# An encoder layer on one core: a bias table moved to the right end of memory, projection weights loaded in pairs, gate stores on another queue, keys loaded by units, and two banks for attention results

## The chip, the cores and the metric

The kernel runs on one core of a Trainium2 chip. A core has a matrix engine (PE, which loads weights, shown as PEld, and streams matmuls), three elementwise engines (DVE, ACT and POOL), and SP, which here only issues transfers (DMAs). Each engine works through its own list of instructions in order and waits on semaphores for the others. Work memory has 128 partitions; results of matmuls go to eight banks of 128 x 512 floats. The metric is the device time of one launch in microseconds (us); a launch is also profiled once, and the profile is what the times of single instructions come from.

## The reference, cut to what matters

One layer over 2048 tokens of width 1024, all in float32:

```python
h = rms_norm(x, norm_mix)
z = h @ w_in            # q_A k_A v_A | q_B k_B v_B | gate_A gate_B
y_a = windowed_gqa(q_a, k_a, v_a, sink)      # |t - s| <= 128, ALiBi, 8 heads in 2 key groups
y_b = neighborhood_attn(q_b, k_b, v_b, rpb)  # 8 x 16 window on a 32 x 64 grid, 8 heads, bias table
gates = sigmoid(concat(g_a, g_b) + b_gate)
merged = gates[:, :1024] * (y_a @ w_proj_a) + gates[:, 1024:] * (y_b @ w_proj_b)
x = x + merged @ w_out
x = x + square(relu(rms_norm(x, norm_mlp) @ w_up)) @ w_down
return rms_norm(x, norm_final)
```

## The kernel before, in words

Matmuls keep float32 accuracy with two halves: an operand is split into a rounded part and the rest, and a product is three matmuls (`mm3`, lines 202 to 204). The split is a CAST on ACT and a subtraction on DVE or POOL.

The kernel has five stages. The first (to about 540 us) multiplies by `w_in` and stores queries, keys, values and half of the gates to DRAM. The second, A, is the windowed attention: 32 units `attn_a(g, i)`, one for a key group g and a block i of 128 queries. The third, B, is the neighbourhood attention: 32 units `attn_b`, four for each of eight heads. The fourth multiplies by `w_proj_b`, merges and multiplies by `w_out`. The fifth is the feed-forward part. The change touches the second and the third, and the order of instructions is the same ahead of them and from the fourth stage's second part on.

A unit of A loads its queries (`qa`), makes scores in a bank `s` (L844, L845), adds the group's table of distances `biasa0` or `biasa1` on DVE (L846), takes exponentials on ACT, divides on POOL (L857), transposes on PE (L863, bank `pt`), splits the result into `ph` and `pl` (L867, L868) and multiplies by the values into a bank `av` (L869, L870), which ACT and DVE empty into `ya` (L872, L873). Group 1 gives the first five units, then all of group 0 runs, then the other eleven of group 1. A unit of B goes the same way with `qb`, keys `kb0` or `kb1` (by the head's parity, 2 MB in three DMAs, L1027 to L1029), values `vb0` to `vb2` (L1040), a bias made by POOL from a loaded piece `braw` (L1012, L1018), and `phb`, `plb`, `av`, `yb`.

Beside the attention PE gets filler work, in steps: `gate_tiles(f)` (128 columns of the gates for two blocks of 512 tokens, 24 matmuls a tile) and `proj_tile(f)` (128 columns of y_a @ w_proj_a for all four blocks, 12 matmuls a tile). The tiles go to a bank `mm`; a gate tile is emptied by a tanh on ACT (L470), and its store to DRAM (`zg`) is issued by ACT; a projection tile is emptied by DVE (L962), multiplied by its gate that was loaded again. The first projections need y_a as four split pages (`y_page`, one for each block of 512 tokens; L939 loads, L282 and L283 split). `paced` ties step n of the filler to a place among the units' transposes: 84 steps in A, 108 in B, of which the last 10 come behind the attention. `put` keeps a store until `flush` issues it on a queue.

The bank tags take 2 (`mm`) + 3 (`s`) + 2 (`pt`) + 1 (`av`) of the eight banks. Pools of work memory are laid from the left end and from the right end, in the order of their lists (L804, L805 for A; L993, L994 for B). B's pools reuse A's places, so a tile of B can be loaded when the last reader of what lay there is done. Before the change kb0 lies over the three `pl` tiles, free space and the end of `ka0`; `kb1` over `sa` and `ya`; `vb0` over the end of `ka1`. With the change kb0 lies over free space, `biasa1` and the end of `ka0`; `kb1` over `sa`, `ya` and `ph`; `vb0` over the end of `ka1` and the first part of `va1`.

Order is set by a scheduler of the language: it takes the program order, the waits that `issue_after` adds and its own idea of durations, and writes one list for each engine.

Of the kernel before, what the change touches and what calls it, by code (L numbers as in the profile page):

```python
# [8 lines left out]
F32 = mybir.dt.float32  # L9
F32R = mybir.dt.float32r  # L10
# [82 lines left out]
def encoder_layer(ctx, tc, x, norm_mix, w_in, b_gate, sink, rpb, w_pa, w_pb, w_out,  # L93
# [374 lines left out]
    def half_tanh(out, z, f):  # L468

        A.activation(out, z, AF.Tanh, scale=0.5, bias=bg[:, f : f + 1])  # L470
# [330 lines left out]
    s_w = ExitStack()  # L801
    wp = pools(s_w, "right", ("raw", "whl", "z"), "w")
    s_a = ExitStack()
    ap_ = pools(s_a, "left", ("dist", "sta", "qa", "biasa1", "ka1", "va1", "sa", "ya", "ph", "pl"), "a")  # L804
    ap_.update(pools(s_a, "right", ("biasa0", "va0", "ka0"), "a"))  # L805

    dist = T(ap_, [P, 384], F32, "dist", 1)
    SY.dma_start(dist, dist_a)
# [20 lines left out]
    def attn_a(g, i):  # L829
        c0, c1 = (1 if i == 0 else 0), (2 if i == 15 else 3)  # L830
        lo, hi = c0 * P, c1 * P
        n = hi - lo
        if bias_a[g] is None:
            make_bias_a(g)
        base = (i - 1) * P
        q = T(ap_, [P, 4, P], F32R, "qa", 3)
        began.append(SY.dma_start(q.bitcast(F32), qs_a[g][i // 8][:, :, i % 8]).ins)
        ka, v = kas[g], vas[g]
        s = T(ap_, [P, 4, 384], F32, "sa", 4)
        st = T(ap_, [P, 8, 4], F32, "sta", 8)  # L840
        mx, nm, sm, es, ri = (st[:, k, :] for k in range(5))
        for h in range(4):
            ps = psum("s", 3)
            PE.matmul(ps[:, :n], q[:, h, :], ka[:, 0, base + lo : base + hi], start=True, stop=False)  # L844
            PE.matmul(ps[:, :n], q[:, h, :], ka[:, 1, base + lo : base + hi], start=False, stop=True)  # L845
            V.tensor_tensor_reduce(out=s[:, h, lo:hi], in0=ps[:, :n], in1=bias_a[g][:, h, lo:hi], scale=1.0,  # L846
                                   scalar=sink_t[:, 4 * g + h : 4 * g + h + 1], op0=ALU.add, op1=ALU.max,
                                   accum_out=mx[:, h : h + 1])
        A.activation(nm, mx, AF.Copy, scale=-1.0)
        V.tensor_tensor(out=es, in0=sink_t[:, 4 * g : 4 * g + 4], in1=mx, op=ALU.subtract)  # L850
        A.activation(es, es, AF.Exp)
        for h in range(4):
            A.activation(s[:, h, lo:hi], s[:, h, lo:hi], AF.Exp, bias=nm[:, h : h + 1], accum_out=sm[:, h : h + 1])
        V.tensor_tensor(out=sm, in0=sm, in1=es, op=ALU.add)
        V.reciprocal(ri, sm)
        for h in range(4):
            G.tensor_scalar(s[:, h, lo:hi], s[:, h, lo:hi], ri[:, h : h + 1], 0.5, ALU.mult, ALU.mult)  # L857
        yield
        po = psum("av", 1)
        for c in range(c0, c1):  # L860
            pt = psum("pt", 2)
            for h in range(4):
                last = PE.transpose(pt[:, h * P : (h + 1) * P], s[:, h, c * P : (c + 1) * P], ident).ins  # L863
# [5 lines left out]
            PE.matmul(po, v[:, i - 1 + c, :], ph, start=c == c0, stop=False)  # L869
            PE.matmul(po, v[:, i - 1 + c, :], pl, start=False, stop=c == c1 - 1)  # L870
        t = T(ap_, [64, 512], F32, "ya", 2)
        A.copy(t, po[64:128, :])  # L872
        V.tensor_tensor(out=t, in0=po[0:64, :], in1=t, op=ALU.add)  # L873
# [44 lines left out]
    def gate_tiles(*fs):  # L918
        raws = [load_slice([(cols(w_in[0], O_GA + f * P), KC)]) for f in fs]
        yield  # L920
        hls = [split_slice(raw) for raw in raws]
        yield
        for b in (3, 2) if len(fs) > 1 else (2, 3):
            for f, hl in zip(fs, hls):
                ps = psum("mm", 2)
                yield from in_chunks(ps, hl, hp[b])
                z = T(wp, [P, 2, BT], F32, "z", 3)[:, 0]
                half_tanh(z, ps, f)
                A.dma_start(zg[b][f // 8][(f % 8) * P : (f % 8 + 1) * P, :], z)
                yield  # L930

    ypages = [None] * NB
# [7 lines left out]
            split(raw, halves(hi)[g], halves(lo)[g], V)  # L940
        ypages[b] = hi, lo

    def proj_tile(f):
        raw = load_slice([(cols(w_pa[0], f * P), 4)])
        yield
        hl = T(wp, [P, 2, KC, P], F32R, "whl", 2)
        split(raw[:, 0:4], hl[:, 0, 0:4], hl[:, 1, 0:4], V)
        yield
        for b in (0, 2):
            z = T(wp, [P, 2, BT], F32, "z", 3)  # L950
            for j in range(2):
                SY.dma_start(z[:, j], zg[b + j][0][f * P : (f + 1) * P, :])
            for j in range(2):
                if ypages[b + j] is None:
                    y_page(b + j)
                hi, lo = ypages[b + j]
                ps = psum("mm", 2)
                for c in range(4):
                    mm3(ps, hl[:, 0, c, :], hl[:, 1, c, :], hi[:, c], lo[:, c], c == 0, c == 3)
                    if c == 1:  # L960
                        yield
                V.scalar_tensor_tensor(out=z[:, j], in0=z[:, j], scalar=1.0, in1=ps, op0=ALU.add, op1=ALU.mult)  # L962
                put(zp[b + j][f], z[:, j])
                yield


    fill = [gate_tiles(f) for f in range(14)] + [gate_tiles(14, 15)] + [proj_tile(f) for f in range(8)]
    for n in (0, 0, 1):
        next(fill[n])
    next(fill[1])  # L970
# [15 lines left out]
    paced(fill, given, 84, 92, 12, last=True)  # L986
# [45 lines left out]
    def attn_b(n_u, h, j, k, bias):  # L1032
# [36 lines left out]
        po = psum("av", 1)  # L1069
        first = True  # L1070
        for pair in range(4):
            pt = psum("pt", 2)
# [78 lines left out]
    first_y = load_y(0)  # L1151
    for _ in range(2):
        next_y = next(first_y)
    paced(fill, given, 108, 128, 4, 10, True)
    flush(queue=SY)
    s_h.close()
    s_pp.close()
# [639 lines left out]
```

## Time and profile before

| | us |
|---|---|
| median of 3 runs | 2664.44 |
| lowest and highest | 2658.15, 2670.09 |
| the profiled execution | 2657.3 |
| its span, first to last instruction | 2655.5 |
| PE busy | 2561.9 |
| DVE busy | 1703.8 |
| ACT busy | 1308.3 |
| mean granted clock of PE | 0.988 |

The span is 1.8 us shorter than the time of the execution that it belongs to. Rows of a timeline read: start, duration, engine, line, operation, written tile <- read tiles, shape, count, and in brackets the idle time of the engine before it with what ended it. A q behind an engine's name means its sequencer, which issues DMAs or waits. The granted clock is the share of the full PE clock; at 0.5 matmuls take twice as long.

### The profile page before, as it was taken

To read this page: it belongs to the slowest core of one execution; us is meant where nothing else is said; L and a number is where in the kernel's file an instruction comes from. 1 tells how busy PE (TensorE), PEld (TensorE's weight loads), DVE (VectorE), ACT (ScalarE), POOL (GpSimd) and SP (SyncE) were. 2 spreads that over 40 slices of the span, in tenths; PEclk is the share of its full clock that TensorE was granted. 3 is DMA by queue.
4 is the path that set the end of the run, shared out by engine and by line. 5 is a ranking of instruction groups with operands and counts; after the bars stand their busy time and mean duration, and the time that the engine had idled before them with its cause. 6 is when DMAs were issued, how large, how long until landed. Compare 5 with 4: busy or idle time off the path is not lost. (4 is left out here: it accounts for less than half of the span.)

```text
span 2655.5 us, 34541 instructions
## 1 busy us (share of the span) xinstructions
PE 2561.9 (96%) x11936; PEld 2124.7 (80%) x11936; DVE 1703.8 (64%) x2700; ACT 1308.3 (49%) x2349; POOL 336.8 (13%) x460
## 2 busy tenths in 40 slices
PE   8999999989996989999999999999999999999998
PEld 6887888878875877878877888888887888888887
DVE  7857477646763556657697776776566634555766
ACT  7365465557763655622336555554444333322444
POOL 1001001043443645300000000000000000000011
PEclk9999999999998999999999999999999999999999
DMA  5768478783347888888888655854436935445555
GB/s 183 224 189 299 144 271 279 243 242 88 102 119 164 221 228 249 231 271 297 284 316 279 225 204 201 286 198 155 147 116 258 326 113 178 143 147 172 185 189 169
DMA packets 348159, 553.21 MB, mean 208 GB/s; under 512 B 30904, under 2 KB 152888, under 8 KB 345808
## 3 DMA queue, kind: packets, MB, share of 16 engines
q1 hardware_dynamic: 328912, 506.96, 59.7%
q10 hardware_dynamic: 15552, 32.51, 3.3%
q0 software_dynamic: 3520, 11.54, 1.2%
q8 instruction: 94, 1.54, 0.2%
q14 instruction: 81, 0.66, 0.1%
HBM read 364.19 MB, written 186.71 MB: 207 GB/s over the span
## 5 line engine op out<-in xcount | busy, mean ns | idle before, releaser
L287 PE MATMUL b<-dwh,dah 128*128 128x512 f32 x896 | 348.7, 389 | 0.4 <-DVE dwh L283 0.4
L288 PE MATMUL b<-dwh,dah 128*128 128x512 f32 x896 | 347.8, 389 | 0.0
L286 PE MATMUL b<-dwh,dah 128*128 128x512 f32 x896 | 338.3, 389 | 1.6 <-ACT dwh L282 1.6
L282 ACT CAST dah<-da 128x1024 fp32r<-128x1024 f32 (+1 forms) x128 | 120.9, 945 | 367.7 <-PE b L288 245.4
L286 PE MATMUL zb<-zh,zwhl 128*128 128x512 f32 x728 | 285.6, 392 | 6.2 <-ACT zb L532 2.4
L287 PE MATMUL zb<-zh,zwhl 128*128 128x512 f32 x728 | 285.2, 392 | 0.0
L288 PE MATMUL zb<-zh,zwhl 128*128 128x512 f32 x728 | 283.8, 391 | 0.9 <-DVE zwhl L283 0.8
L283 DVE TENSOR_TENSOR dah<-da,dah 128x1024 fp32r<-128x1024 f32 (+1 forms) x128 | 139.1, 1089 | 217.3 <-ACT dah L282 214.4
L286 PE MATMUL b<-ubh,uwhlb 128*128 128x512 f32 x592 | 231.5, 391 | 5.0 <-ACT uwhlb L282 3.4
L287 PE MATMUL b<-ubh,uwhlb 128*128 128x512 f32 x592 | 231.1, 390 | 0.0
L288 PE MATMUL b<-ubh,uwhlb 128*128 128x512 f32 x592 | 229.3, 389 | 0.0
L286 PEld LDWEIGHTS b<-dwh,dah 128*128 128x128 f32 x896 | 168.1, 188 | 36.9 <-ACT dwh L282 2.1
L287 PEld LDWEIGHTS b<-dwh,dah 128*128 128x128 f32 x896 | 168.2, 188 | 35.7 <-DVE dwh L283 0.8
L288 PEld LDWEIGHTS b<-dwh,dah 128*128 128x128 f32 x896 | 168.2, 188 | 34.8
L279 DVE TENSOR_TENSOR uc<-b,uc 128x512 f32<-128x512 f32 x160 | 109.2, 688 | 119.3 <-PE b L288 112.7
L202 PE MATMUL mm<-zh,whl 128*128 128x512 f32 x384 | 165.8, 432 | 7.3 <-ACT zh L282 7.3
L286 PEld LDWEIGHTS zb<-zh,zwhl 128*128 128x128 f32 x728 | 137.0, 188 | 38.9 <-ACT zb L532 3.3
L288 PEld LDWEIGHTS zb<-zh,zwhl 128*128 128x128 f32 x728 | 137.0, 188 | 29.7 <-DVE zwhl L283 1.7
L287 PEld LDWEIGHTS zb<-zh,zwhl 128*128 128x128 f32 x728 | 137.0, 188 | 27.6
L203 PE MATMUL mm<-zh,whl 128*128 128x512 f32 x384 | 152.3, 397 | 1.5 <-DVE zh L283 1.5
L204 PE MATMUL mm<-zh,whl 128*128 128x512 f32 x384 | 152.4, 397 | 0.0
L286 PEld LDWEIGHTS b<-ubh,uwhlb 128*128 128x128 f32 x592 | 111.7, 189 | 29.5 <-ACT uwhlb L282 3.8
(249 smaller groups left out, 5657.0 us busy)
## 6 DMA issues: line engine op xcount, KB each, us to landing
at<-uc SPq DMA_DIRECT2D x224, 256.0 KB
da<-at SPq DMA_DIRECT2D x96, 512.0 KB
dw<-in_w_down_dram SPq DMA_DIRECT2D x160, 256.0 KB
uraw<-in_w_up_dram SPq DMA_DIRECT2D x32, 1024.0 KB
pgl<-wo_d SPq DMA_DIRECT2D x28, 1024.0 KB
zraw<-in_w_in_dram SPq DMA_DIRECT2D x24, 1024.0 KB
z<-zg SPq DMA_DIRECT2D x64, 256.0 KB
qs_a<-ze SPq DMA_DIRECT2D x32, 256.0 KB
```

The source lines that it names most:

```text
L202: PE.matmul(ps, lh, rh, start=first, stop=False)
L203: PE.matmul(ps, lh, rl, start=False, stop=False)
L204: PE.matmul(ps, ll, rh, start=False, stop=last)
L279: return eng.tensor_tensor(out=out, in0=a, in1=b, op=op).ins
L282: A.copy(hi, src)
L283: return eng.tensor_tensor(out=lo, in0=src, in1=hi.bitcast(F32), op=ALU.subtract).ins
L286: PE.matmul(ps, lh, rh, start=first, stop=False, skip_group_check=True)
L287: PE.matmul(ps, lh, rl, start=False, stop=False, skip_group_check=True)
L288: PE.matmul(ps, ll, rh, start=False, stop=last, skip_group_check=True)
```

## The change

It does six things. `biasa1` goes from the left pools to the right ones, last in their list. `proj_tiles(f)` takes two features: one tile `raw` and one split serve f and f + 1, both started at the generator's second step. A gate's two blocks share one tile `z`, and its stores go through `put` to SP. A's later keys are loaded in three pieces, tied to the begin of its 4th, 9th and 14th unit. `av` has two banks and `mm` one (the four projection tiles with f = 6 and 7 on blocks 2 and 3 use `s`). The last 14 of B's 108 filler steps come behind the attention, not 10.

```diff
-    ap_ = pools(s_a, "left", ("dist", "sta", "qa", "biasa1", "ka1", "va1", "sa", "ya", "ph", "pl"), "a")
-    ap_.update(pools(s_a, "right", ("biasa0", "va0", "ka0"), "a"))
+    ap_ = pools(s_a, "left", ("dist", "sta", "qa", "ka1", "va1", "sa", "ya", "ph", "pl"), "a")
+    ap_.update(pools(s_a, "right", ("biasa0", "va0", "ka0", "biasa1"), "a"))
...
-        po = psum("av", 1)
+        po = psum("av", 2)
...
         for b in (3, 2) if len(fs) > 1 else (2, 3):
             for f, hl in zip(fs, hls):
-                ps = psum("mm", 2)
+                ps = psum("mm", 1)
                 yield from in_chunks(ps, hl, hp[b])
-                z = T(wp, [P, 2, BT], F32, "z", 3)[:, 0]
-                half_tanh(z, ps, f)
-                A.dma_start(zg[b][f // 8][(f % 8) * P : (f % 8 + 1) * P, :], z)
+                if f not in zs:
+                    zs[f] = T(wp, [P, 2, BT], F32, "z", 3)
+                half_tanh(zs[f][:, b - 2], ps, f)
+                put(zg[b][f // 8][(f % 8) * P : (f % 8 + 1) * P, :], zs[f][:, b - 2])
                 yield
...
-    def proj_tile(f):
-        raw = load_slice([(cols(w_pa[0], f * P), 4)])
-        yield
-        hl = T(wp, [P, 2, KC, P], F32R, "whl", 2)
-        split(raw[:, 0:4], hl[:, 0, 0:4], hl[:, 1, 0:4], V)
+    def proj_tiles(f):
+        yield
+        hl = split_slice(load_slice([(cols(w_pa[0], (f + i) * P), 4) for i in range(2)]), V)
         yield
         for b in (0, 2):
-            z = T(wp, [P, 2, BT], F32, "z", 3)
...
+            for i in range(2):
+                z = T(wp, [P, 2, BT], F32, "z", 3)
+                for j in range(2):
+                    SY.dma_start(z[:, j], zg[b + j][0][(f + i) * P : (f + i + 1) * P, :])
+                for j in range(2):
...
+                    ps = psum("mm", 1) if f + b < 8 else psum("s", 3)
...
-    drive((attn_a(g, i) for g, i in units_a[:2]), live, False)
-    load_kv(0, 0)
-    drive((attn_a(g, i) for g, i in units_a[2:8]), live, False)
-    with tc.issue_after(began[5]):
-        load_kv(0, 1)
-        load_kv(1, 1)
-    drive((attn_a(g, i) for g, i in units_a[8:14]), live, False)
+    at = 0
+    for n, g, m in ((4, 0, 0), (9, 0, 1), (14, 1, 1)):
+        drive((attn_a(*u) for u in units_a[at:n]), live, False)
+        with tc.issue_after(began[n - 1]):
+            load_kv(g, m)
+        at = n
...
-    paced(fill, given, 108, 128, 4, 10)
+    paced(fill, given, 108, 128, 4, 14)
```

What the scheduler makes of it shows at the border of A and B. On PE, before the change, A's last products stand ahead of B's first scores (`s` from `kb0`); numbers behind a name tell the tiles apart:

```order
L870 MATMUL av_370_7008<-pl_808_7037,va1_478_4522 128x512
L863 MATMUL pt_376_7058<-ident_63,sa_794_6939 128x128 x4
L869 MATMUL av_374_7046<-ph_810_7052,va1_478_4522 128x512
L870 MATMUL av_374_7046<-pl_811_7053,va1_478_4522 128x512
L869 MATMUL av_374_7046<-ph_812_7063,va1_478_4522 128x512
L870 MATMUL av_374_7046<-pl_813_7064,va1_478_4522 128x512
L1050 MATMUL s_388_7520<-kb0_841_7497,qb_844_7507 128x288
```

Now these scores stand between products of A's last units; this piece, in A's third last unit, begins at the end of the filler tile mm_386 and ends where mm_387 begins in the same bank:

```order
L204 MATMUL mm_386_7346<-zh3_305_2946,whl_821_7258 128x512
L869 MATMUL av_366_6966<-ph_792_6972,va1_478_4522 128x512
L870 MATMUL av_366_6966<-pl_793_6973,va1_478_4522 128x512
L863 MATMUL pt_369_6989<-ident_63,sa_770_6793 128x128 x4
L1049 MATMUL s_388_7510<-kb0_831_7487,qb_834_7497 128x288
L1049 MATMUL s_389_7515<-kb0_831_7487,qb_834_7497 128x384
L1049 MATMUL s_390_7520<-kb0_831_7487,qb_834_7497 128x384
L869 MATMUL av_366_6966<-ph_794_6983,va1_478_4522 128x512
L870 MATMUL av_366_6966<-pl_795_6984,va1_478_4522 128x512
L863 MATMUL pt_371_7005<-ident_63,sa_780_6864 128x128 x4
L202 MATMUL mm_387_7377<-zh1_279_2740,whl_824_7316 128x512
```

These are the second halves of the scores s_388 to s_390; their first halves stand 14 rows earlier, ahead of mm_386's last six matmuls. On SP, before the change, the loads of kb0 come behind A's last stores (`y_a`), and vb0's load long before them:

```order
L1040 DMA vb0_848_7517<-vs_b0_92 96x4x256
L175 DMA y_a1_143<-ya_782_6862 64x4x128
L175 DMA y_a1_143<-ya_792_6933 64x4x128
L189 DMA raw_1084_8902<-in_w_in_dram 128x8x128
L175 DMA y_a1_143<-ya_802_7004 64x4x128
L175 DMA y_a1_143<-ya_809_7042 64x4x128
L1012 DMA braw1_855_7551<-tab1_153 128x1x512
L1027 DMA kb0_841_7497<-ks_b0_88 128x2048
```

Now kb0's loads stand ahead of A's last stores, behind a gate's store (`zg`):

```order
L175 DMA y_a1_143<-ya_768_6787 64x4x128
L175 DMA zg21_103<-z_825_7344 128x512
L1026 DMA kb0_831_7487<-ks_b0_88 128x2048
L1027 DMA kb0_831_7487<-ks_b0_88 64x2048
L1028 DMA kb0_831_7487<-ks_b0_88 64x2048
L175 DMA y_a1_143<-ya_778_6858 64x4x128
```

and vb0's load, with kb1's behind it, stands at the end of A's stores:

```order
L175 DMA y_a1_143<-ya_805_7038 64x4x128
L1039 DMA vb0_838_7507<-vs_b0_92 96x4x256
L1011 DMA braw1_845_7541<-tab1_153 128x1x512
L1039 DMA vb1_847_7548<-vs_b0_92 96x4x256
L1039 DMA vb2_854_7583<-vs_b0_92 128x4x256
L175 DMA zg31_105<-z_828_7402 128x512
L175 DMA y_a1_143<-ya_810_7065 64x4x128
L189 DMA raw_1073_8889<-in_w_in_dram 128x8x128
L1026 DMA kb1_868_7669<-ks_b0_88 128x2048
```

So vb0 changed places with kb0: the keys moved ahead of A's last stores, the values of B's first unit behind them.

More of the change, by code (lines that the diff above doesn't have):

```diff
@@ L920, in gate_tiles @@
         yield
-        hls = [split_slice(raw) for raw in raws]
+        hls, zs = [split_slice(raw) for raw in raws], {}
         yield
@@ L941, in y_page @@
         ypages[b] = hi, lo
-    def proj_tile(f):
-        raw = load_slice([(cols(w_pa[0], f * P), 4)])
+    def proj_tiles(f):
         yield
-        hl = T(wp, [P, 2, KC, P], F32R, "whl", 2)
-        split(raw[:, 0:4], hl[:, 0, 0:4], hl[:, 1, 0:4], V)
+        hl = split_slice(load_slice([(cols(w_pa[0], (f + i) * P), 4) for i in range(2)]), V)
         yield
         for b in (0, 2):
-            z = T(wp, [P, 2, BT], F32, "z", 3)
[L951 to L960, printed above, removed]
-                        yield
[L962 to L967, printed above, removed]
+            for i in range(2):
[3 more added lines that the diff above has]
+                for j in range(2):
+                    if ypages[b + j] is None:
+                        y_page(b + j)
+                    hi, lo = ypages[b + j]
+                    ps = psum("mm", 1) if f + b < 8 else psum("s", 3)
+                    for c in range(4):
+                        cc = 4 * i + c
+                        mm3(ps, hl[:, 0, cc, :], hl[:, 1, cc, :], hi[:, c], lo[:, c], c == 0, c == 3)
+                        if c == 1:
+                            yield
+                    V.scalar_tensor_tensor(out=z[:, j], in0=z[:, j], scalar=1.0, in1=ps, op0=ALU.add, op1=ALU.mult)
+                    put(zp[b + j][f + i], z[:, j])
+                    yield
+    fill = [gate_tiles(f) for f in range(14)] + [gate_tiles(14, 15)] + [proj_tiles(f) for f in range(0, 8, 2)]
     for n in (0, 0, 1):
@@ L1068, in attn_b @@
         flush(queue=SY)
-        po = psum("av", 1)
+        po = psum("av", 2)
         first = True
@@ L1153, in encoder_layer @@
         next_y = next(first_y)
-    paced(fill, given, 108, 128, 4, 10, True)
+    paced(fill, given, 108, 128, 4, 14, True)
     flush(queue=SY)
```

## The prediction

> **What bounds the kernel now.** The first part of the page says that the kernel is a stream of matmuls, so that only idle PE or a slow PE clock can be won back:
>
> ```profile
> PE 2561.9 (96%) x11936; PEld 2124.7 (80%) x11936; DVE 1703.8 (64%) x2700; ACT 1308.3 (49%) x2349; POOL 336.8 (13%) x460
> ```
>
> The two programs stand in the same order ahead of the attention (about 540 us) and again from the merge stage on (about 1240 us), so I cut the time between by windows (start, end, length; PE busy and its count; granted clock; DMA share; GB/s).
>
> ```profile
> 566.00:783.00 217.00, 211.15 (x1111) 0.99 0.42 116
> 783.00:810.00 27.00, 25.57 (x136) 1.00 0.27 78
> 810.00:870.00 60.00, 38.42 (x201) 0.80 0.89 199
> 870.00:950.00 80.00, 79.93 (x499) 1.00 0.78 208
> 950.00:1050.00 100.00, 85.70 (x472) 0.91 0.87 242
> 1050.00:1150.00 100.00, 99.70 (x622) 1.00 0.80 236
> 1150.00:1180.00 30.00, 26.18 (x111) 0.94 0.74 248
> ```
>
> Three windows lose time: 810 to 870 (60 − 38.4 = 21.6 us idle), 950 to 1050 (14.3) and 1150 to 1180 (3.8). Each also has a clock below 1. In the full-clock windows of the second attention an instruction takes 79.93/499 = 99.70/622 = 0.160 us; 201 of them would be 32.2, not 38.4, so the slow clock after the stall costs 6.2 us more; likewise 85.70 − 472 × 0.160 = 10.1 us. The losses are 27.8, 24.4 and about 5.6 us (3.8 and 6% of 30). The view of waits of PE, 540 to 1250 us, names them (total, times, longest):
>
> ```profile
> PE s L1050 <- DMA kb<-ks_b: 16.0, 2, 11.8
> PE mm L202 <- ACT zh L282: 7.3, 2, 3.8
> PE s L844 <- DMA qa<-qs_a: 5.9, 1, 5.9
> PE av L869 <- DVE ya L873: 5.8, 5, 1.9
> PE s L1050 <- DMA qb<-qs_b: 5.3, 1, 5.3
> PE b L202 <- ACT pgr L1147: 3.8, 2, 3.7
> PE av L1090 <- ACT phb L1084: 2.0, 1, 2.0
> PE av L1090 <- DVE yb L1098: 0.8, 1, 0.8
> ```
>
> **Table of biases to the right end.** The largest wait is for the keys of the first head of the second attention. PE's timeline:
>
> ```profile
> 780.17 0.60 PE L863 MATMUL pt<-ident,sa 128*128 128x128 f32 x4
> 780.53 0.48 PE L202 MATMUL mm<-zh,whl 128*128 128x512 f32 x1
> ...
> 783.49 0.28 PE L845 MATMUL s<-ka,qa 128*128 128x256 f32 x1
> ...
> 797.12 0.39 PE L204 MATMUL mm<-zh,whl 128*128 128x512 f32 x1
> 797.35 0.39 PE L202 MATMUL mm<-zh,whl 128*128 128x512 f32 x1
> ...
> 810.19 0.40 PE L870 MATMUL av<-pl,va 128*128 128x512 f32 x1
> 822.34 1.25 PE L1050 MATMUL s<-kb,qb 128*128 128x288 f32 x3 [11.75 <-DMA kb<-ks_b]
> 827.87 6.08 PE L1050 MATMUL s<-kb,qb 128*128 128x288 f32 x21 [4.29 <-DMA kb<-ks_b]
> ...
> 845.66 2.71 PE L1050 MATMUL s<-kb,qb 128*128 128x384 f32 x6 [5.29 <-DMA qb<-qs_b]
> ```
>
> and the rows of SP's queue, DVE and POOL that belong to it:
>
> ```profile
> 783.80 0.61 SPq L1040 DMA_DIRECT2D vb<-vs_b  x1
> ...
> 810.03 0.62 SPq L1012 DMA_DIRECT2D braw<-tab  x1
> 810.82 0.34 SPq L1027 DMA_DIRECT2D kb<-ks_b  x1
> ...
> 824.53 0.34 SPq L1027 DMA_DIRECT2D kb<-ks_b  x1
> ```
>
> ```profile
> 783.81 0.48 DVE L846 CUSTOM_DVE_ANT_0 sa<-s,biasa,sink_t 128x256 f32<-128x256 f32 x1 [0.98 <-PE s L845]
> ```
>
> ```profile
> 816.23 3.78 POOL L1018 TENSOR_TENSOR biasl<-braw,masks 128x384 f32<-128x384 f32 x3 [19.14 <-DMA braw<-tab]
> ```
>
> Now kb0 lies over the pl tiles, which are read until 810.19, and is asked for 0.6 us later; its first transfer is there 11.5 us after the issue, the others 17.0 us after it (827.87). In the changed layout it lies over free space and biasa1, whose last reader is the DVE row at 783.81. SP's rows ahead of it are done by then, so I take 785.4 for the issue and 796.9 for the first part. The 17.0 us were taken with 0.9 MB of values behind the 2 MB of keys, which now come later; I take 14, 799.4 for the rest. In the new order PE has 25 matmuls 512 wide (0.23 us start to start, 797.12 to 797.35) and 12 transposes (0.36 for four, 780.17 to 780.53) from the last score to its first row on kb0: 6.8 us, so it comes there at 790.3 and waits 6.6 us, in the middle of A's tail instead of behind it. The second halves of these scores stand 3.2 us of work later, at 800.1, when the rest is there: nothing.
>
> Two things become late in its place. vb0 could be loaded at 783.80; it now lies over va1, read until A's last product. Between that and the first use of vb0 PE has 2.1 us of work (six 512-wide matmuls and ten transposes). A small load here takes 6 us from issue to use (the table braw, issued 810.03, is used by POOL at 816.23), 384 KB behind nothing perhaps 5.6: wait 3.5 us. And kb1, which is asked for 14.3 us behind A's last product now (824.53 against 810.19), because it waits for A's last store: with the 11.5 and 17.0 us of transfer and 17 us until PE needs it (13.5 of work, 3.5 of the wait before) I take 6 us, if the store lands in 8.5 us since no 2 MB of keys are ahead of it. The wait for qb goes: its load stands far ahead of its use in the new order. Sum of idle time 16.1 against 21.6, clock loss in proportion 4.6 against 6.2: **−7 us**, bounds −27.8 (all of it) and +8 (kb1 late by its full 14.3).
>
> **Two banks for the results, one for the filler.** The attention's result bank was single (now two), the filler's double (now one). Rows of the views by line (minimum/median/maximum ns; then who waits for the DVE add that empties a result):
>
> ```profile
> L470 ACT ACTIVATE z<-mm,bg x32: 667/687/702, 546.3 to 964.2; 128x512 f32<-128x512 f32 x32
> ```
>
> ```profile
>   PEld av L869: 8.2, 9
>   PE av L869: 5.8, 5
> ```
>
> With two result banks the 5.8 and 0.8 us of the waits table go: **−6.6**; bound 0. What the filler pays is not in the trace, since its second bank hides it. Between the last matmul of one filler tile and the first of the next, the new order has about 2 us of other matmuls (in the excerpt shown 2.1 us); emptying takes 0.69 us and whatever stands before it on ACT or DVE. The nearest row is the single result bank: there 64 handovers, with two instructions in a row to empty it and mostly 2.4 to 3.8 us of work between, cost 6.6 us, 0.10 each. Some 60 handovers at that price: **+6**. Bounds: 0, and 60 × 0.69 = 41 us if nothing hides the emptying.
>
> **Projection weights in pairs, late.** Eight loads and splits of weights become four of twice the size, on no path. What counts is the four pages of y_a that the first projections need: a pair of features now uses pages 0 and 1 twice before page 2 is touched. In the new order 16 us of PE work lie between the first rows on page 1 and on page 2, before it was 6. The stalls there:
>
> ```profile
> 970.77 0.38 PE L1090 MATMUL av<-phb,vb 128*128 128x256 f32 x1 [1.99 <-ACT phb L1084]
> ...
> 981.03 0.80 PE L202 MATMUL mm<-zh,whl 128*128 128x512 f32 x1 [3.52 <-ACT zh L282]
> ...
> 1021.35 0.80 PE L202 MATMUL mm<-zh,whl 128*128 128x512 f32 x1 [3.75 <-ACT zh L282]
> ```
>
> ```profile
> 969.71 0.33 ACTq L929 DMA_DIRECT2D zg<-z  x1
> 970.13 0.97 ACT L1084 CAST phb<-pt 128x512 fp32r<-128x512 f32 x2 [4.70 <-DMA kb<-ks_b]
> ```
>
> The 3.75 us belongs to a later page and goes; the 3.52 of the first page stays, since its load stands right behind 2 MB of keys in the new order. The gates' store on ACT's queue is the row at 969.71: ACT stood 4.70 us around it, and PE 1.99 us for the next CAST on ACT. On SP it holds no engine, so this goes too. With its share of the slow clock (10.1 × 5.74/14.3 = 4.1): **−9.8**; bounds −24.4 and +10, should the same pages collide with keys and 32 more stores in SP's queue. Elsewhere those 32 stores take 0.33 us each from ACT, which is not the bound; on SP each is flushed behind a finished result, so it does not hold the loads behind it long: 0. [...]
>
> **Tail of 14 steps, and keys by units.** Four more half tiles of the projection (6 matmuls each, 24 × 0.23 = 5.5 us) stand behind the last attention unit. That covers the wait for the first y page:
>
> ```profile
> 1169.25 0.50 PE L202 MATMUL b<-pgr,whl 128*128 128x512 f32 x1 [3.66 <-ACT pgr L1147]
> ```
>
> 3.8 us with 6% of 30 us of clock: **−5.5**; bound 0. The four steps leave an attention that is full (0.1 and 0.3 us idle in its other windows), at no cost. Keys by units: the fourth qa load now stands ahead of ka0's 1.5 MB, the fifth behind it. The 5.94 us wait should move to the fifth unit, about as long: 0, bounds −6 and +4.
>
> **The sum**: −7 − 6.6 + 6 − 9.8 − 5.5 = −22.9 us. The profiled execution took 2657.3 us and would take 2634.4. It is 7.1 us below the median of the three runs (2664.44), which spread from 2658 to 2670; against the median I forecast 2641.5, say **2642**. A change under 0.5% (13.3 us) is about what a measurement of this kernel can't tell from none.
>
> **Rivals.**
> 1. The waits only move on. kb0, vb0 and kb1 together cost the 27.8 us of today, and the pages their 24.4: −6.6 + 6 − 5.5 = −6, 2658. For it: the same megabytes cross the same queue, at a DMA share of 0.87 to 0.89 in both windows. Against it: keys leave 25 us earlier, at a share of 0.27.
> 2. The boundary closes: kb0 comes in time, kb1 in 11 us, and only some 4 us remain of 27.8: −40, 2624. For it: the DMA share of 0.27 in 783 to 810, while the 11.5 us were taken at 0.89.
> 3. Slower: the single filler bank. Every handover shows the emptying: 41 in place of 6 us, and the boundary and the pages give half of 16.8: 35 + 8 − 23 = +20, 2685. It decides from 29/60 = 0.48 us a handover, where the rest of the sum is gone. For it: what empties a bank stands in order behind other work on DVE and ACT, busy 64% and 49% of the span. Against it: the 64 handovers of the single result bank cost 0.10 us each.
> 4. Slower by the clock: the short waits at the single bank let the granted clock fall as the waits at 970.77, 981.03 and 1021.35 did; 10.1 us for 14.3 idle there, so 0.7 us more for each us of wait; with 30 us of such waits, 24 over the forecast, and 21 for the clock, 45 − 23 = +22, 2686. Against it: the first attention has waits of up to 1.9 us at a clock of 0.99. [...]
>
> **How the numbers follow.** Forecast 0.48, rival 1 0.20, rival 2 0.14, rival 3 0.12, rival 4 0.06. The range 2620 to 2668 takes in the forecast's own (2628 to 2656) with rivals 1 and 2, and leaves out rivals 3 and 4. Faster by over 0.5%: 0.46 of the forecast's and rival 2's 0.14, less a rest at the border, 0.59; slower 0.18; within 0.5% 0.23.
>
> **What would show it.** In the changed profile: score matmuls on kb0 between A's last products, one wait of 5 to 8 us for kb there and shorter ones for vb and kb1; no PE wait for ya or yb; new PE waits of filler matmuls on ACT z and DVE z, under 10 us in all; one wait on ACT zh, not two; none on pgr; the clock of 810 to 870 near 0.85. I am wrong if filler waits pass 25 us, if the window behind 950 us is no better, or if kb1 takes what kb0 gave.

## The result, and the profile after

The changed kernel takes 2634.39 us (median of four runs, 2628.92 to 2635.17) against 2661.36 (four runs of the kernel before on the same chip): ratio 0.9889, 95% interval 0.986 to 0.9918. It is faster: the medians fell by 27 us, where 22.9 were forecast. Its profiled execution took 2633.67 us with a span of 2631.9, 23.6 less than before; the work of PE is the same, and its busy time, which the slow clock stretches (matmuls 512 wide start 0.43 us apart at a granted clock of 0.50, 0.23 at 1.00), is 5.0 us less, at a mean granted clock of 0.993 against 0.988:

```profile
PE 2556.9 (97%) x11936; PEld 2123.0 (81%) x11936; DVE 1708.3 (65%) x2696; ACT 1308.2 (50%) x2345; POOL 335.1 (13%) x460
```

The windows of PE that the prediction read, now (start, end, length; PE busy and its count; granted clock; DMA share; GB/s):

```profile
566.00:783.00 217.00, 212.05 (x1122) 1.00 0.43 122
783.00:810.00 27.00, 26.65 (x139) 1.00 0.54 143
810.00:870.00 60.00, 53.45 (x318) 0.97 0.96 247
870.00:950.00 80.00, 73.84 (x447) 0.96 0.83 231
950.00:1050.00 100.00, 96.64 (x573) 0.96 0.87 244
1050.00:1150.00 100.00, 97.95 (x550) 1.00 0.76 248
1150.00:1180.00 30.00, 23.64 (x95) 0.89 1.04 364
```

The border of A and B (810 to 870) went from 38.4 to 53.5 us of busy PE in 60. The stretch 950 to 1050 gained 10.9, but 870 to 950 lost 6.1, and 1150 to 1180 lost 2.5. The waits of PE in the same part of the program say what stands there now (total, times, longest):

```profile
PE b L202 <- DVE z L1553: 6.4, 1, 6.4
PE s L1049 <- DMA kb<-ks_b: 4.5, 2, 4.3
PE av L1089 <- ACT phb L1083: 4.2, 2, 3.0
PE av L1089 <- DVE plb L1084: 3.4, 7, 1.0
PE s L844 <- DMA qa<-qs_a: 3.3, 1, 3.3
PE mm L202 <- ACT z L470: 2.2, 2, 1.7
PE av L869 <- ACT ph L867: 2.1, 3, 1.2
PE av L1089 <- DMA vb<-vs_b: 1.8, 2, 1.4
...
PE mm L202 <- DVE z L963: 1.1, 1, 1.1
```

The waits for `zh`, `ya`, `yb` and `pgr` are gone by name. Those for `phb` and `plb` grew from 2.3 to 7.6 us. New are `ph`, a few for the filler's bank (`z` of L470 and L963, 3.3 us in all) and, the largest, 6.4 us at the start of the fourth stage.

For all runs I worked out from the traces the loss in four stretches: the idle time of PE, and the time that matmuls took above the usual spacing of their shape in the same execution (the slow clock). The kernels do the same matmuls with the same total of work, so the sums can be compared; between stretches some work moves. Each row is one execution, which need not be its kernel's median one: the profile of after_tail10_pages_in_place is 8 us above the median of its runs, before_table_right's 7 and after_banks_before's 6 above, after_own_gate_tiles' 7 below, after_table_left's and after_pages_in_place's 5 below. So a few us between two rows are a hint, and the times decide.

| loss of PE, us | 540 to 783 | 783 to 870 | 870 to 1050 | 1050 to 1240 | sum |
|---|---|---|---|---|---|
| before | 20.8 | 28.4 | 24.6 | 8.2 | 82.0 |
| changed | 16.4 | 10.7 | 19.4 | 12.7 | 59.1 |
| after_table_left | 16.1 | 23.6 | 14.4 | 16.0 | 70.0 |
| before_table_right | 24.2 | 9.3 | 30.7 | 9.7 | 73.9 |
| after_banks_before | 24.4 | 11.8 | 22.0 | 5.7 | 63.9 |
| after_tail10 | 18.9 | 10.9 | 25.4 | 3.6 | 58.8 |
| after_gates_act | 19.3 | 11.7 | 20.2 | 14.9 | 66.0 |
| after_proj_single | 18.2 | 11.7 | 26.3 | 6.0 | 62.2 |
| after_keys_before | 18.1 | 11.3 | 19.4 | 12.7 | 61.5 |
| after_pages_early | 18.6 | 11.2 | 21.8 | 12.9 | 64.5 |
| after_pages_in_place | 16.8 | 12.3 | 22.6 | 14.2 | 66.0 |
| after_tail10_pages_early | 19.8 | 10.5 | 22.9 | 2.8 | 56.0 |
| after_tail10_pages_in_place | 20.0 | 13.6 | 28.8 | 2.6 | 65.0 |
| after_own_gate_tiles | 18.0 | 10.0 | 20.8 | 1.8 | 50.6 |

So of the 22.9 us that the changed kernel's execution won, 17.7 come from the border, 5.2 from the stretch of the y_a pages, 4.4 from A, and the end gives 4.5 back.

### The profile page after: what moved, and what is told of

Its sections match the earlier page's. It is cut to its first block, busy times and chain, and to the rows that moved or that the text cites. A ratio compares the mean times of both kernels' runs of the same rounds, so it can differ in the third digit from the quotient of the medians.

```text
span 2631.9 us, 34511 instructions
## 1 busy us (share of the span) xinstructions
PE 2556.9 (97%) x11936; PEld 2123.0 (81%) x11936; DVE 1708.3 (65%) x2696; ACT 1308.2 (50%) x2345; POOL 335.1 (13%) x460
## 4 chain that ended last, share of the span: by engine, by line
PE 78%; DMA 10%; DVE 6%; ACT 3%; issue 2%; SPq 2%; POOL 0%; DVEq 0%; ACTq 0%; POOLq 0%
PE b L287 16%; PE b L288 16%; PE b L286 16%; PE zb L286 5%; PE zb L288 5%; PE zb L287 5%; PE mm L202 2%; PE mm L204 2%; PE mm L203 2%; PE av L1089 1%; DMA h2d<-ht 1%; PE pt L863 1%; DMA y_b<-yb 1%; PE pt L1077 1%; PE s L1049 1%
## 5 line engine op out<-in xcount | busy, mean ns | idle before, releaser
L202 PE MATMUL mm<-zh,whl 128*128 128x512 f32 x368 | 158.5, 431 | 3.3 <-ACT z L470 2.2
L204 PE MATMUL mm<-zh,whl 128*128 128x512 f32 x368 | 146.1, 397 | 0.0
L203 PE MATMUL mm<-zh,whl 128*128 128x512 f32 x368 | 146.0, 397 | 0.0
```

Of the source, the lines that this page charges most:

```text
L202: PE.matmul(ps, lh, rh, start=first, stop=False)
L203: PE.matmul(ps, lh, rl, start=False, stop=False)
L204: PE.matmul(ps, ll, rh, start=False, stop=last)
```

## The experiments

Twelve kernels ran, in four groups, each group with its own runs of the kernel before on the same chip (medians 2665.36, 2662.27, 2665.04 and 2663.34 us). The ratios, always to those runs, are what is compared; 0.001 is 2.7 us. The changed kernel's own is 0.9889 (0.986 to 0.9918).

### The table of biases, both ways

after_table_left, the change without its first part:

```diff
-    ap_ = pools(s_a, "left", (..., "qa", "ka1", "va1", ...), "a")
-    ap_.update(pools(s_a, "right", ("biasa0", "va0", "ka0", "biasa1"), "a"))
+    ap_ = pools(s_a, "left", (..., "qa", "biasa1", "ka1", "va1", ...), "a")
+    ap_.update(pools(s_a, "right", ("biasa0", "va0", "ka0"), "a"))
```

> The changed kernel with biasa1 back among the left pools and nothing else undone. Theory 'table': the place of the table alone lets the first keys of the second attention load 25 us earlier, so without it the wait for kb before the first score comes back (about 12 + 4 us, with the slow clock behind it some 17 us in all), and the time is 15 to 20 us above the changed kernel, 2650 to 2655 us. Rival 'order': the gain comes from the new order as a whole (banks, pairs, tail), the keys only move a wait; then the time is less than 8 us above the changed kernel.

Measured: 2650.28 us, ratio 0.9944 (0.9928 to 0.996). before_table_right is the same edit alone, on the kernel before (the diff read the other way round):

> The kernel before with biasa1 moved to the right end and nothing else. Theory 'table': 13 to 20 us faster than before, 2642 to 2649 us, with scores on kb0 standing between the last products of the first attention. Rival 'order': under 8 us faster.

Measured: 2650.15 us, ratio 0.9934 (0.9915 to 0.9953). One edit of two lines is worth 15 us by the medians and 18 by the ratio on its own, and 16 and 15 as a part of the whole. The window 810 to 870 of after_table_left, and its waits for the keys and for qb:

```profile
810.00:870.00 60.00, 46.66 (x253) 0.86 0.88 211
```

```profile
PE s L1049 <- DMA kb<-ks_b: 9.6, 2, 5.6
PE s L1049 <- DMA qb<-qs_b: 6.8, 1, 6.8
```

Here kb0 lies over the `pl` tiles again, is issued at 805.57 instead of 779.28 us, and with the wait for qb the border loses 23.6 us in place of 10.7. In before_table_right the border is as good as in the changed kernel:

```profile
810.00:870.00 60.00, 54.27 (x306) 0.97 0.81 205
```

So the order of the loads, which the place in memory decides, is the cause, and it needs no other part of the change. (In its profiled execution, the slowest of six, the stretch 870 to 1050 lost 6 us more than in the kernel before: PE's waits for `zh` and `phb` were 8.8 and 5.3 us there, against 7.3 and 2.0.)

### Two banks for results, one for the filler

after_banks_before:

```diff
-        po = psum("av", 2)
+        po = psum("av", 1)
...
-                ps = psum("mm", 1)
+                ps = psum("mm", 2)
```

> The changed kernel with one result bank and two filler banks, as before. Theory as predicted: the second result bank is worth 6.6 us and the lost filler bank costs 6 at most 3 by the changed profile's waits (2.2 + 1.1 us), so this is 0 to 5 us slower than the changed kernel, with the waits for ya back and those for ACT z and DVE z gone. Rival: the single filler bank is what costs; this is 5 us or more faster than the changed kernel.

Measured: 2638.16 us, ratio 0.9902 (0.9887 to 0.9918). That is 3.8 us above the changed kernel by the medians and 3.5 by the ratios, and the intervals overlap: a gain from the new banks is not shown, and there is no sign that the single bank of the filler costs. The run changes both banks at once, so it doesn't part the two. With the old ones the waits for `ya` and `yb` are back (6.8 us in four waits, 3.9 in three) and A's loss rises to 24.4 us; with the new ones it is 16.4.

### The tail of the filler

after_tail10, two numbers:

```diff
-    paced(fill, given, 108, 128, 4, 14)
+    paced(fill, given, 108, 128, 4, 10)
```

> The changed kernel with 10 filler steps behind the attention, not 14. Theory as predicted: the tail covers the wait for the first split page of y_b, so with 10 the wait there (6.4 us in the changed profile) grows by up to 5.5 us and the time by 3 to 6 us. Rival: the wait there is set by the chain from the last attention unit over stores, loads and splits, and the steps fill the attention as well as its end: no difference beyond 2 us, or a gain.

Measured: 2633.69 us, ratio 0.9883 (0.9868 to 0.9899): no difference. But the loss moved: the end of B is better with 10 (3.6 us in place of 12.7) and the stretch of the pages worse (25.4 for 19.4). Its windows, and PE's longest wait with the ACT row ahead of it:

```profile
950.00:1050.00 100.00, 89.97 (x532) 0.95 0.91 258
...
1150.00:1180.00 30.00, 30.00 (x134) 1.00 1.06 368
```

```profile
961.29 0.80 PE L202 MATMUL mm<-zh,whl 128*128 128x512 f32 x1 [6.15 <-ACT z L470]
```

```profile
959.60 1.04 ACT L282 CAST zh<-raw 128x1024 fp32r<-128x1024 f32 x1 [7.02 <-DMA raw<-y_a]
960.55 0.68 ACT L470 ACTIVATE z<-mm,bg 128x512 f32<-128x512 f32 x1
```

The name "ACT z" in PE's wait looks like the filler's single bank. ACT's own row shows that it stood 7.02 us in the CAST ahead, for a page of y_a: the tanh that empties the bank is behind it in ACT's list. In the changed kernel the same happens under the name `phb`:

```profile
946.59 1.04 ACT L282 CAST zh<-raw 128x1024 fp32r<-128x1024 f32 x1 [5.24 <-DMA raw<-y_a]
947.54 0.58 ACT L1083 CAST phb<-pt 128x512 fp32r<-128x512 f32 x1
```

```profile
948.17 0.58 PE L1089 MATMUL av<-phb,vb 128*128 128x256 f32 x1 [2.97 <-ACT phb L1083]
```

And in the changed kernel's end of B, PE, DVE and SP read:

```profile
1158.38 0.79 PE L202 MATMUL b<-pgr,whl 128*128 128x512 f32 x1 [6.37 <-DVE z L1553]
```

```profile
1135.73 0.69 DVE L963 SCALAR_TENSOR_TENSOR z<-z,mm 128x512 f32<-128x512 f32 x1 [0.43 <-PE mm L204]
...
1157.63 2.09 DVE L1553 SCALAR_TENSOR_TENSOR z<-z,b 128x512 f32<-128x512 f32 x3 [8.71 <-DMA z<-zg]
```

```profile
1139.60 0.42 SPq L175 DMA_DIRECT2D zp<-z  x1
...
1149.60 4.16 SPq L1544 DMA_DIRECT2D z<-zg  x4
```

The last projection of the tail ends in `z` at 1136.4 us and its store goes out at 1139.60; the three `z` tiles are also what the fourth stage loads its gates into, and the second of these loads is issued only at 1149.60. That the wait comes from this was a guess until the last run below.

### Projections one feature at a time

after_proj_single takes back the pairs:

```diff
-            for i in range(2):
-                z = T(wp, [P, 2, BT], F32, "z", 3)
...
+            z = T(wp, [P, 2, BT], F32, "z", 3)
...
-    fill = ... + [proj_tiles(f) for f in range(0, 8, 2)]
+    fill = ... + [proj_tile(f) for f in range(8)]
```

> The changed kernel with projections of one feature again (weights loaded and split one feature at a time, all four pages of y_a touched by the first feature). Theory 'pages', the prediction's: with pairs a page's stall is spread over twice the work, so without them a page wait as long as before (3.75 us, with clock 5 to 7) comes back: 2639 to 2643, and ACT waits longer for loads of y_a than the 14.1 us between 870 and 1050 us of the changed kernel. Rival 'moved': the stall on the pages is in the changed kernel too, only behind the waits for phb and plb, and the pairs change nothing: 2632 to 2637.

Measured: 2641.41 us, ratio 0.9932 (0.991 to 0.9954), as 'pages' had it, with an interval that just touches the changed kernel's. PE stops twice, for 12.75 us:

```profile
953.98 0.58 PE L1090 MATMUL av<-phb,vb 128*128 128x256 f32 x1 [4.80 <-ACT phb L1084]
...
1000.71 0.80 PE L202 MATMUL mm<-zh,whl 128*128 128x512 f32 x1 [7.95 <-ACT zh L282]
```

The loss of 870 to 1050 is 26.3 us against 19.4, and ACT's wait for y_a there 21.7 against 14.1. At the end it gets 6.7 us back (6.0 for 12.7); why was not tried.

### The gates' stores on ACT

after_gates_act:

```diff
-                put(zg[b][f // 8][(f % 8) * P : (f % 8 + 1) * P, :], zs[f][:, b - 2])
+                A.dma_start(zg[b][f // 8][(f % 8) * P : (f % 8 + 1) * P, :], zs[f][:, b - 2])
```

> The changed kernel with the gates' stores issued by ACT again, directly behind the tanh; all else as changed (2634.4 us). Theory 'ACT stall', the prediction's: a store on ACT's queue can hold ACT for some us (4.70 us in the kernel before) and PE behind it; the stall comes back with its clock: 2636 to 2640. Rival 'nothing': ACT is not the bound and the place of the stores does not matter: 2632 to 2637, no gap of ACT above 4 us ahead of a CAST that stands behind a store. Rival 'SP': the 32 stores on SP delay loads that stand behind them (pages of y_a, keys), so that taking them off SP makes it faster: 2626 to 2631.

Measured: 2638.28 us, ratio 0.9915 (0.9895 to 0.9936). The time falls into the range of 'ACT stall', but the trace doesn't show its mechanism: behind the stores in B, ACT waits 1.7 us at most for anything but matmuls and the splits of y_a, and the stretch 870 to 1050 loses 20.2 us against 19.4. The stall itself is in other traces. In before_table_right, with its stores on ACT, the tanh ends at 889.4, the store leaves six us later, and the CAST behind it is late by as much:

```profile
895.39 0.34 ACTq L929 DMA_DIRECT2D zg<-z  x1
895.82 0.48 ACT L1084 CAST phb<-pt 128x384 fp32r<-128x384 f32 x1 [6.42 <-DMA y_b<-yb]
```

Where the 4 us by the medians, 7 by the ratios, come from, in intervals that overlap, stays open. The longest wait that this trace has and the changed kernel's hasn't is one of PE for values (`vb`), 3.9 us near 1049 us; it is not the stores' doing, since after_keys_before and after_own_gate_tiles, with their stores on SP, have 2.6 and 3.4 us there.

### A's keys

after_keys_before:

```diff
-    for n, g, m in ((4, 0, 0), (9, 0, 1), (14, 1, 1)):
-        drive((attn_a(*u) for u in units_a[at:n]), live, False)
-        with tc.issue_after(began[n - 1]):
-            load_kv(g, m)
-        at = n
+    drive((attn_a(g, i) for g, i in units_a[:2]), live, False)
+    load_kv(0, 0)
+    drive((attn_a(g, i) for g, i in units_a[2:8]), live, False)
+    with tc.issue_after(began[5]):
+        load_kv(0, 1)
+        load_kv(1, 1)
+    drive((attn_a(g, i) for g, i in units_a[8:14]), live, False)
```

> The changed kernel with the first attention's keys loaded as before (first piece of group 0 behind two units, the other two tied to the sixth unit). The prediction's theory: no difference, 2631 to 2637, a wait for qa of 3 to 6 us in either order. Rival: the new order of keys is what brought the wait for qa from 5.94 to 3.26 us and took some clock with it: 2637 to 2642, with the wait for qa near 6 us.

Measured: 2638.84 us, ratio 0.9895 (0.9878 to 0.9913). By the ratio it is the changed kernel's time, by the median 4 us above: between the two expectations. The wait for qa decides against the rival:

```profile
549.84 0.55 PE L844 MATMUL s<-ka,qa 128*128 128x256 f32 x1 [3.43 <-DMA qa<-qs_a]
```

It stays near 3 us with the old order of keys, so its fall from 5.94 us is no merit of the new one.

### Pages of y_a earlier

after_pages_early separates the load of a page from its split and issues it two filler steps ahead:

```diff
+        if f == 0:
+            y_load(0)
         yield
...
+                    n = (b + j + 1) % NB
+                    if i == (0 if j == 0 else 1) and n and n not in yraws:
+                        y_load(n)
```

> The changed kernel with the loads of the four y_a pages issued two filler steps ahead of their split, the first ones then ahead of the 2 MB of keys of the fifth head. Theory 'late pages': the splits of these pages on ACT wait for their loads (14.1 us between 870 and 1050 us in the changed kernel), and what stands behind them on ACT and DVE makes PE wait under other names (phb, plb, z: some 7.7 us) with the slow clock that follows; with early loads most of the loss of 19.4 us in this stretch goes: 2622 to 2628. Rival 'not the loads': the waits for phb and plb have another cause, or the early loads push the keys back and PE waits for kb instead: 2631 to 2638.

Measured: 2638.54 us, ratio 0.9919 (0.9897 to 0.994); 'late pages' missed. A page is loaded in two halves. Those of page 0 went out at 852 and 879 us and those of page 1 at 920 and 929, all ahead of the keys at 936. ACT still waited 12.8 us for y_a, 7.4 of them in one piece for page 2, whose first half went out at 939.20, behind these keys:

```profile
952.90 1.04 ACT L282 CAST zh<-raw 128x1024 fp32r<-128x1024 f32 x1 [7.39 <-DMA raw<-y_a]
```

And PE's longest wait in the stretch was not for a page:

```profile
1047.68 0.55 PE L1099 MATMUL av<-phb,vb 96*128 96x256 f32 x1 [6.00 <-DMA vb<-vs_b]
```

The changed kernel's profile has no such wait there. The same pages with a tail of 10, after_tail10_pages_early:

> As the run with early pages, and with a tail of 10 steps in place of 14. The run with a tail of 10 alone had 3.6 us of loss behind 1050 us in place of 12.7, but 25.4 in place of 19.4 from 870 to 1050, of which one wait of 6.15 us behind a late page. Theory 'late pages' and 'tail of 14 holds the z tiles' together: both losses go, 2616 to 2624, faster than with a tail of 14. Rival 'moved on': the end of the second attention is set by its last unit in any case, the same as with the tail of 14 within 3 us.

Measured: 2631.86 us, ratio 0.9891 (0.9871 to 0.9911): the gain forecast did not come. ACT waited 6.0 us for page 1 and 9.6 for the second half of page 2, which went out at 956.89, behind keys issued at 950. Then after_pages_in_place loads the pages into their own low halves, so that no `raw` tile is needed:

```diff
-            raw = T(wp, [P, KC, P], F32, "raw", 3).rearrange(...)
-            SY.dma_start(raw, y_a[g][:, b * BT : (b + 1) * BT].rearrange(...))
-            split(raw, halves(hi)[g], halves(lo)[g], V)
+            SY.dma_start(halves(lo)[g].bitcast(F32), y_a[g][:, b * BT : (b + 1) * BT].rearrange(...))
...
+            split(halves(lo)[g].bitcast(F32), halves(hi)[g], halves(lo)[g], V)
```

> The changed kernel with the y_a pages loaded straight into the low half's page and split in place, so that they need no tile raw; pages 0 and 1 are then issued ahead of the sixth 2 MB of keys, which stood ahead of page 1 in the changed kernel and in the run with early pages (there ACT still waited 7.4 us for page 1). Theory 'late pages': ACT's waits for loads of y_a between 870 and 1050 us fall from 14.1 us to under 7, the wait of 3 to 5 us for phb near 950 us goes, and the loss of 19.4 us there falls to 8 to 13: 2624 to 2631. Rival 'moved on': the keys behind the pages come late instead, or another wait on phb stands there with the pages in time: 2632 to 2640.

Measured: 2643.37 us, ratio 0.9919 (0.9899 to 0.9939), and after_tail10_pages_in_place:

> The same with a tail of 10. By 'late pages' the loss of 25.4 us between 870 and 1050 us in the run with a tail of 10 falls by 8 to 14 while the 3.6 us behind 1050 stay: 2618 to 2626, faster than both kernels. Rival 'moved on': 2629 to 2636.

2637.97 us, ratio 0.9894 (0.9874 to 0.9914). Both lie above both of the ranges expected. The first expectation takes the late page of after_pages_early for page 1; by the order of its eight loads it was page 2. In after_pages_in_place pages 0 and 1 now go out at 915 and 921 us, ahead of the keys, and cost ACT 2.0 us at most (with the tail of 10, 6.9); the next two pages stand behind the same keys. SP, ACT and PE of after_pages_in_place:

```profile
938.97 0.62 SPq L1039 DMA_DIRECT2D kb<-ks_b  x1
...
948.04 2.08 SPq L938 DMA_DIRECT2D zh<-y_a  x1
```

```profile
957.99 1.04 ACT L282 CAST zh<-zh 128x1024 fp32r<-128x1024 f32 x1 [3.91 <-DMA zh<-y_a]
```

```profile
960.30 0.58 PE L1102 MATMUL av<-phb,vb 128*128 128x256 f32 x1 [4.65 <-ACT phb L1096]
```

An earlier load also brings its split earlier into ACT's list, and the wait moves from page 1 to page 2. PE's wait for `vb` is there too, 2.9 us. So by the trace 'moved on' holds, though the times are longer than it had them; what this stretch would lose without any pages was not tried.

### Tiles of its own for the fourth stage's gates

after_own_gate_tiles changes the tile into which the fourth stage loads its gates, and leaves the order of matmuls alone:

```diff
-    p4.update(pools(s_pg, "right", ("z",), "m"))
+    p4.update(pools(s_pg, "right", ("z", "zgm"), "m"))
...
-            g, ga = T(wp, [P, 2, BT], F32, "z", 3), T(p4, [P, 2, BT], F32, "z", 2)
+            g, ga = T(p4, [P, 2, BT], F32, "zgm", 3), T(p4, [P, 2, BT], F32, "z", 2)
```

> The changed kernel with three tiles of their own for the gates that the fourth stage loads, in place of the three z tiles, which the projections of the tail hold until their stores have landed; the matmuls stand in the same order, and the loads of the first three gates now stand ahead of the tail on SP. Theory 'held tiles': the wait of 6.4 us for DVE z L1553 near 1158 us (the run with a tail of 10 has none) comes from the tail of 14 holding the z tiles; it goes, and with its clock the loss behind 1050 us falls from 12.7 to 3 to 6: 2624 to 2629, the fastest so far. Rival 'other loads': the weights and pages that are loaded at the same place are as late, so PE waits there for whl or pgr instead: 2631 to 2637.

Measured: 2631.09 us (2623.70 to 2634.28), ratio 0.9868 (0.9842 to 0.9894). The windows at the end of B, and all that PE waits for from 1050 to 1260 us:

```profile
1050.00:1150.00 100.00, 98.73 (x566) 1.00 0.79 253
1150.00:1180.00 30.00, 30.00 (x134) 1.00 1.07 377
```

```profile
PE mm L202 <- DVE z L963: 0.9, 1, 0.9
PE av L1089 <- DVE plb L1084: 0.2, 1, 0.2
```

The wait of 6.4 us is gone and nothing took its place: the shared `z` tiles were its cause. With tiles of their own the first three gates are loaded at 1098 us, ahead of the tail on SP, so the run doesn't part the wait for a free tile from the place in SP's list. Nor do 14 steps always cost this much: after_banks_before and after_proj_single, with the same tail, lose 5.7 and 6.0 us there. Two of the six runs took 2623.7 us, one of them the profiled one, four 2630.4 to 2634.3, so the median misses its range and lies in that of 'other loads', whose waits the trace doesn't show. It has the lowest median of the kernels tried, and is faster than before; that it beats the changed kernel is not shown, since the intervals overlap.

## Why the prediction was right, and where it was not

The sum of −22.9 us met a loss that fell by 22.9 and a span that fell by 23.6. For the median, 2642 us were forecast and 2634.39 measured. The close match of the sum is luck: two terms were wrong by 10 us each, in opposite directions. Of the signs it named, scores on kb0 between A's last products, the end of the waits for ya, yb and pgr, and filler waits under 10 us came; the wait of 5 to 8 us for kb0, the one wait on zh by name and the clock near 0.85 in 810 to 870 (0.97) did not.

- **The table, −7.** The mechanism was right, the size was not: 17.7 us were won at the border, and the edit alone gives 15. The rows of the changed kernel, SP and then PE:

```profile
779.28 0.33 SPq L1026 DMA_DIRECT2D kb<-ks_b  x1
...
810.24 0.60 SPq L1039 DMA_DIRECT2D vb<-vs_b  x1
...
821.68 0.33 SPq L1026 DMA_DIRECT2D kb<-ks_b  x1
```

```profile
785.92 0.76 PE L1049 MATMUL s<-kb,qb 128*128 128x288 f32 x3
...
789.89 0.72 PE L1049 MATMUL s<-kb,qb 128*128 128x288 f32 x3 [0.26 <-DMA kb<-ks_b]
...
813.92 0.38 PE L1089 MATMUL av<-phb,vb 96*128 96x256 f32 x1 [1.45 <-DMA vb<-vs_b]
...
831.97 0.90 PE L1049 MATMUL s<-kb,qb 128*128 128x288 f32 x2 [4.27 <-DMA kb<-ks_b]
```

  The step that failed is "its first transfer is there 11.5 us after the issue". The first scores ran 6.6 us after the issue without waiting, the second halves 10.6 us after it. A itself also ran 5 us earlier (its last scores at 778.2 us, before at 783.3). So the 6.6 us for kb0 became 0.26. vb0 was there after 3.7 us, not 5.6, and PE waited 1.45 in place of 3.5; kb1 cost 4.27 in place of 6, and the clock 3.8 in place of 4.6. The truth is nearer to rival 2 than to the forecast, but rival 2's argument doesn't hold either: the share of 0.27 is a mean over 783 to 810, and the first transfer ran from 779.28 to 785.92. In that time the DMA share was 0.93 here; from the issue to the first scores it was 0.94 in the kernel before, and 0.92 in after_table_left, where PE had the first keys 5.6 us after the issue. What differed is the rate, 282 and 266 GB/s against 200 in the kernel before; why it was lower there, and so why the first keys took 11.5 us, stays open.

- **Two banks, −6.6 and +6.** The filler's bank: 3.3 us by the names (2.2 and 1.1) in place of 6, and 1.73 of it was a late page: ACT's CAST ahead of that tanh had waited 2.03 us for y_a. The results' bank: the waits for `ya` and `yb` went, but in A `ph`, `pl` and `sta` took 4.5 us (2.1, 1.1 and 1.3), where `pl` and `sta` had 1.2 before, so its term was too large as well. Together −0.6 was forecast. A lost 4.4 us less in these two executions, but by the time of the run with the old banks a gain is not shown. Rivals 3 and 4 did not come.

- **The pages, −9.8.** The stretch 870 to 1050 gained 5.2. The step that failed is "the 3.75 us belongs to a later page and goes": it changed its name. ACT's waits for y_a in that stretch fell only from 16.3 to 14.1 us, and PE met them as `phb`, `plb` and `z`. That the pairs help is supported by after_proj_single, whose six runs all took longer than the changed kernel's four. That the store on ACT's queue was a part of it isn't shown.

- **The tail, −5.5.** Wrong in sign by the trace, where the end of B lost 4.5 us more, and nothing by the time of after_tail10. The wait on `pgr` was covered, as forecast; what the working left out is what the four more steps hold. The `z` tiles are shared with the fourth stage, and they come free later now. I named what is late next at the border, and did not ask it here.

- **Keys by units, 0.** No difference shown. The wait for qa did not move to a later unit, as forecast, but from 565 to 550 us, and fell from 5.94 to 3.26. With the old order of keys it is at 550 too, with the old banks at 566 with 2.9 us; so neither made it shorter, and what did stays open.

## What to carry to other kernels

The place of a tile in memory sets the order of loads: ask for each large load which last reader frees its bytes, and how far that is ahead of the first use; here that one question was worth 15 us. Take the landing time of a transfer from several loads, not from one (here the same first piece of keys was used 11.5, 6.6 and 5.6 us after its issue, at DMA shares of 0.94, 0.93 and 0.92), and when a step is moved later, list the buffers that it holds and who wants them next. A wait that vanishes by name is not gone until the engine that was named has been followed back through its own list.

## What the runs showed of the hardware

Half clock came in steps in these traces. A window of the changed kernel at half clock with those on either side of it (columns as above), and one of the kernel before at half clock:

```profile
1149.00:1155.90 6.90, 3.01 (x14) 1.00 1.07 374
1155.90:1162.73 6.83, 4.35 (x10) 0.50 1.09 361
1162.73:1170.00 7.27, 7.27 (x33) 1.00 1.02 373
```

```profile
811.50:831.98 20.48, 5.33 (x16) 0.50 1.02 215
```

These stretches last 6.83 and 20.48 us. The shortest one of the changed kernel, 831.66 to 835.08 us, lasts 3.41 (granted clock 0.50, and 1.00 in the 3.41 us on either side). In the changed kernel half clock begins at 831.7, 923.8, 947.7, 971.6 and 1155.9 us between 540 and 1250: these times lie 27, 7, 7 and 54 times 3.413 us apart, and the two stretches shown are 2 and 6 times that long. At half clock matmuls 512 wide start 0.43 us apart (changed kernel, 1159.39 to 1162.38), at full clock 0.23 (1163.02 to 1165.99): 1.9 times, where the section on time and profile says twice.

I divided the profiled executions of the kernel before and of the changed kernel (540 to 1250 us) into steps of 3.413 us, each on the grid that its own starts of half clock make, and counted by the share of a step in which PE idled. At full clock, half clock followed none of the 374 steps with less than 0.3, one of the 7 with 0.31 to 0.43, two of the 4 with 0.50 to 0.54 and all 9 with 0.62 or more. At half clock it went on after all 10 steps with 0.37 or more and after none of the 12 with 0.10 or less. So in these two executions what a wait cost went with how much of one step PE idled: around the one of 1.73 us at 923.58 it was 0.51 (920.41 to 923.82), and a step at half clock followed; around the one of 1.45 at 813.92 it was 0.42 (811.18 to 814.59), and none did. The two waits for qa differ in the same way. The 3.43 us in after_keys_before go from 546.41 to 549.84, and the 512-wide matmuls behind them start 0.43 us apart until 552.96 and 0.23 from 553.32 on; by these starts half clock ended near 553.2, so the wait filled the step ahead of it, if that was 3.41 us long too. The 3.26 us in the changed kernel lie across a border at 548.36, with PE idle 0.52 of the step ahead of it and 0.43 of the one behind, and the clock was 1.00 in both. The prediction's "in proportion" is only a mean.
